# Weight differences tied to a later weight tile, and the last layer's value product as three 256-column matmuls

## The chip, the core and the metric

The kernel runs on one core of one Trainium2 chip. The metric is the device time of one launch in microseconds (us), the median of several executions. Engines are named as in the profile: PE (TensorE matmul) and PEld (its weight loads), DVE (VectorE), ACT (ScalarE), POOL (GpSimd), SP (SyncE, which issues the weight stream's DMAs).

## The reference

A two-layer encoder trunk over 272 tokens (16 meta tokens and 256 others) of width 2048, in float32. What matters here is the second half of each layer, the feed-forward part with inner width 5632:

```python
h2 = _rmsnorm(h_stream, norm_ffn[i])
up = h2 @ w_up[i]
u_gate = _dwconv3_centred(up[..., :D_FF], w_conv[i], b_conv[i])
u_val = up[..., D_FF:]
h_stream = h_stream + (jax.nn.silu(u_gate) * u_val) @ w_down[i]
```

The first half of a layer is grouped attention beside a Fourier branch, both gated and projected. The meta tokens are dropped at the end, so the last layer needs 256 columns of the value product.

## The kernel before, in words

**Precision.** Every float32 product is split in two parts. A weight tile `raw` (512 KB, four k-tiles by 256 output columns) is fetched by SP, copied on ACT into a rounded high part `wh` (the cast in `split_w`), and DVE subtracts to get the low part `wl`. The activations lie as a high and a low part too (`xHL`, `gHL`, `mH`/`mL`, `qH`/`qL`). One k-tile of one output tile is then three matmuls: `wh` by high, `wh` by low, `wl` by high. Activations are the moving operand of 272, 258 or 256 columns; 128 x 128 blocks of the weights are the stationary one, loaded anew by each matmul.

**Pairs.** Where high and low part together fit into 512 columns, `group` can issue two matmuls: `wh` by both parts side by side (512 columns) and `wl` by high (256 columns). The caller asks for it by handing over one moving operand in place of two. The two halves of the result then have to be added behind it. In the last layer (`fused`) the value product `uv` and the down products `d`, but for the last of them, are done like that.

**The stream.** `order` is a list of all weight tiles in the order of use. `advance` and `pump` keep the splits two tiles ahead of PE and the fetches four more. There are three buffers each for `wh` and `wl`, so the cast of tile i+2 can run when PE has finished tile i-1. A tile lasts 24 matmuls in a group of three. After every sixth matmul `step()` is called, four times a tile; it advances the side work, which is written as generators that say after how many steps they want to go on. All engines work their instructions off in the order in which the program was written.

**The weight sums.** For the last layer's down projection the first 32 of 44 k-tiles are done by a scheme with seven products per 2 x 2 block in place of eight. It needs differences of weight blocks, four for each of 16 block sets (`NPR`). The generator `weight_sums` makes them during the feed-forward part of layer 0: ACT issues a load of a 512 KB block into `b0` to `b3` (a one-element copy from the weight tile in use ahead of it ties it to that place in the stream), nine steps later DVE is given the subtraction, two steps later ACT is given the store into a DRAM tile `ts`. Layer 1 fetches the `ts` tiles back in its weight stream, and its products are called `ps_x`.

**Placement.** Tiles come from pools that are laid out one behind another: `per`, `wp`, `small`, and behind these `mix` (first half of a layer) and `ffn` (second half). The tables `X_AT`, `Q_AT`, `G_AT`, `FR_AT` and `WL_AT` say at which column within its tile a part begins.

Of the kernel before, what the change touches and what calls it, by code (L numbers as in the profile page):

```python
# [10 lines left out]
F32 = mybir.dt.float32  # L11
F32R = mybir.dt.float32r
AF = mybir.ActivationFunctionType
ALU = mybir.AluOpType
AX = mybir.AxisListType

P = 128
D = 2048
# [17 lines left out]
NPR = sum(FF_SPLIT[-1][:2]) // 2  # L36
# [17 lines left out]
X_AT, Q_AT, G_AT = ((44, 12), (24, 40)), ((44, 4), (8, 24)), ((12, 44), (0, 0))  # L54
# [1 line left out]
WL_AT.update({(0, k): 16 for k in ("q", "k", "v", "f", "f01", "ga", "gf", "ug", "uv", "d")})  # L56
FR_AT = 12
WL_AT.update({(l, "s"): 40 for l in range(2)})
WL_AT.update({(1, k): 16 for k in ("q", "ga", "gf", "a", "o", "ug")})
BLK = ((0, 16), (16, 144), (144, 272))  # L60

C_COS, C_SIN, C_MASK = 0, T, 2 * T
# [58 lines left out]
def encoder_kernel(ctx, tc, xT, params, consts, bmat, w_in, w_abr, w_four, w_f64, w_out, w_up, w_down, w_blk, outT):  # L121
    nc = tc.nc
# [98 lines left out]
    def split_w(i, a, b, eng=None):  # L221
        if i not in splits:
            h = wp.tile([P, CW, MG * P], F32R, tag="wh", name=f"wh{i}")
            lo = wp.tile([P, CW * MG * P + 64], F32R, tag="wl", name=f"wl{i}")
            o = wl_at[i]
            splits[i] = h, lo[:, o:o + CW * MG * P].rearrange("p (c m) -> p c m", c=CW)
        h, lo = splits[i]
        r = raws[i]
        if eng is None:
            nc.scalar.copy(h[:, a:b], r[:, a:b])  # L230
        else:
            eng.tensor_copy(h[:, a:b], r[:, a:b])
        nc.vector.tensor_tensor(lo[:, a:b], r[:, a:b], h[:, a:b].bitcast(F32), op=ALU.subtract)  # L233
        if b == CW:
            del raws[i]
# [283 lines left out]
    for l in range(DEPTH):  # L519
# [447 lines left out]
        with tc.tile_pool(name=f"ffn{l}", bufs=1) as fp:  # L967
# [2 lines left out]

            def weight_sums():
                tt = nc.vector.tensor_tensor
                for q in range(NPR):
                    b = [fp.tile([P, D // 2], F32, tag=f"b{e}", name=f"b{e}") for e in range(4)]
                    for e, sums in ((0, ()), (1, ((0, 1, 0, 0),)), (3, ((1, 3, 1, 1), (3, 3, 0, 2))), (2, ((2, 2, 3, 3),))):
                        nc.scalar.copy(b[e][:, 0:1], st["cur"][:, 0, 0:1].bitcast(F32))
                        nc.scalar.dma_start(b[e], w_blk[2 * q + e // 2, e % 2])
                        yield 9
                        for o, x, y, to in sums:
                            tt(b[o], b[x], b[y], op=ALU.subtract)  # L980
                            yield 2
                            nc.scalar.dma_start(tsum[q][to], b[o])
                        yield 3

            sets, prods = [], {"have": {}}
            if last:
# [83 lines left out]
            def both(t_, k, at):  # L1070
                a, n = at[0] + lo2, XP + at[1] - at[0]
                if n == XP:
                    return t_[:, k, :, a:a + W2]
                b = 2 * XP * k + a
                s = min(b, 2 * XP * t_.shape[1] - 2 * n)
                return t_.rearrange("p k r n -> p (k r n)")[:, s:s + 2 * n].rearrange("p (r n) -> p r n", r=2)[:, :, b - s:b - s + W2]

            k0 = 0
            for c, n in enumerate(FF_SPLIT[l]):
                whole = last and c < 2  # L1080
                if not last:
                    gHL = fp.tile([P, FF_SPLIT[l][0], 2, XP], F32R, tag="gHL", name="gHL")
                    gH, gL = (gHL[:, :, e, G_AT[l][e]:G_AT[l][e] + T] for e in range(2))
                    gp = lambda k: both(gHL, k, G_AT[l])
                elif whole:
                    gs = fp.tile([P, GN if c == 0 else n * SEQ], F32, tag=f"g{c}", name=f"g{c}")
                    sets.append(gs[:, :n * SEQ].rearrange("p (k t) -> p k t", t=SEQ))
                else:
                    gs = fp.tile([P, GN], F32R, tag="g0", name="gHL")[:, G_LAST:G_LAST + n * 2 * SEQ].rearrange("p (k e t) -> p k e t", e=2, t=SEQ)
                    gH, gL = gs[:, :, 0], gs[:, :, 1]  # L1090
                    gp = lambda k: gs[:, k]
                at_ = NM if last else 0
                if last and c:
                    push(combos(c - 1), 2)
                for i in range(k0 // MG, (k0 + n) // MG):
                    ps = group((l, "ug", i), xr(lo), W)
                    if i == 0:
                        drain()
                    cs = []
                    for m in range(MG):  # L1100
                        mt = 2 * i + m
                        wc = lambda t: prm[:, P_CW + (l * 3 + t) * FT + mt:P_CW + (l * 3 + t) * FT + mt + 1]
                        bc = prm[:, P_CB + l * FT + mt:P_CB + l * FT + mt + 1]
                        u = fp.tile([P, T], F32, tag="u", name="u", bufs=3)
                        nc.vector.tensor_tensor(u[:, lo:T], ps[m][:, :W], rstdB[:, lo:T], op=ALU.mult)
                        cv = fp.tile([P, T], F32, tag="cv", name="cv", bufs=4)
                        nc.scalar.activation(cv[:, lo2:T], u[:, lo2:T], AF.Identity, bias=bc, scale=wc(1))
                        a = max(lo2, 1)
                        nc.vector.scalar_tensor_tensor(cv[:, a:T], u[:, a - 1:T - 1], wc(0), cv[:, a:T], op0=ALU.mult, op1=ALU.add)
                        nc.vector.scalar_tensor_tensor(cv[:, lo2:T - 1], u[:, lo2 + 1:T], wc(2), cv[:, lo2:T - 1], op0=ALU.mult, op1=ALU.add)  # L1110
                        nc.scalar.activation(cv[:, lo2:T], cv[:, lo2:T], AF.Silu)
                        nc.vector.tensor_tensor(cv[:, lo2:T], cv[:, lo2:T], rstdB[:, lo2:T], op=ALU.mult)
                        cs.append(cv)
                    ps = group((l, "uv", i), (lambda kt: (both(xHL, kt, X_AT[l]),)) if fused else xr(lo2), W2)
                    for m in range(MG):
                        j = 2 * i + m - k0
                        cv = cs[m]
                        val = ps[m][:, :W2]
                        if fused:
                            v = fp.tile([P, W2], F32, tag="v", name="v", bufs=2)  # L1120
                            nc.scalar.copy(v, ps[m][:, W2:2 * W2])
                            nc.vector.tensor_tensor(v, v, val, op=ALU.add)
                            val = v
                        if whole:
                            nc.vector.tensor_tensor(sets[c][:, j, :], cv[:, lo2:T], val, op=ALU.mult)
                            continue
                        nc.vector.tensor_tensor(cv[:, lo2:T], cv[:, lo2:T], val, op=ALU.mult)
                        h_ = gH[:, j, lo2 - at_:T - at_]
                        nc.scalar.copy(h_, cv[:, lo2:T])
                        nc.vector.tensor_tensor(gL[:, j, lo2 - at_:T - at_], cv[:, lo2:T], h_.bitcast(F32), op=ALU.subtract)  # L1130
                lastc = c == len(FF_SPLIT[l]) - 1
                k0 += n
                if whole:
                    continue
                if last:
                    drain()
                    push(turned(), 2)
                for mg in range(8):
                    two = fused and not (lastc and mg == 7)
                    ps = group((l, "d", c, mg), (lambda kt: (gp(kt),)) if two  # L1140
                               else (lambda kt: (gH[:, kt, lo2 - at_:T - at_], gL[:, kt, lo2 - at_:T - at_])), W2)
                    if last and mg == 0:
                        drain()
                    for m in range(MG):
                        mt = 2 * mg + m
                        if two:
                            nc.vector.tensor_tensor(XT[:, mt, lo2:T], XT[:, mt, lo2:T], ps[m][:, W2:2 * W2], op=ALU.add)
                        if last and lastc:
                            ot = fp.tile([P, SEQ], F32, tag="ot", name="ot", bufs=3)
                            nc.vector.tensor_tensor(ot, XT[:, mt, NM:T], ps[m][:, :W2], op=ALU.add)  # L1150
                            nc.scalar.dma_start(outT[mt * P:(mt + 1) * P, :], ot)
                        else:
                            nc.vector.tensor_tensor(XT[:, mt, lo2:T], XT[:, mt, lo2:T], ps[m][:, :W2], op=ALU.add)
                            if lastc:
                                norm_in(mt, P_NM + (l + 1) * KT)
# [54 lines left out]
```

## Time and profile before

| what | value |
|---|---|
| time, median of 3 runs | 2530.25 us (2529.61 to 2532.1) |
| the profiled execution, its own time | 2528.11 us |
| its span | 2526.0 us |
| granted TensorE clock, mean | 0.999 |
| busy: PE, DVE, ACT | 99%, 73%, 51% |
| HBM traffic over the span | 218 GB/s |

PE's busy share counts matmuls that overlap in the pipeline, so it says that PE hardly ever has nothing to do, not that each matmul goes as fast as it can. What tells the speed of a run of matmuls is the distance from one start to the next. Start times in the timeline are in us from the start of the span; a duration there is that of one instruction from entering to leaving the engine, longer than that distance.

### The profile page before, as it was taken

To read this page: it belongs to the slowest core of one execution; us is meant where nothing else is said; L and a number is where in the kernel's file an instruction comes from. 1 tells how busy PE (TensorE), PEld (TensorE's weight loads), DVE (VectorE), ACT (ScalarE), POOL (GpSimd) and SP (SyncE) were. 2 spreads that over 40 slices of the span, in tenths; PEclk is the share of its full clock that TensorE was granted. 3 is DMA by queue.
4 is the path that set the end of the run, shared out by engine and by line. 5 is a ranking of instruction groups with operands and counts; after the bars stand their busy time and mean duration, and the time that the engine had idled before them with its cause. 6 is when DMAs were issued, how large, how long until landed. Compare 5 with 4: busy or idle time off the path is not lost.

```text
span 2526.0 us, 47879 instructions
## 1 busy us (share of the span) xinstructions
PE 2511.2 (99%) x19404; PEld 2441.2 (97%) x19404; DVE 1852.2 (73%) x2851; ACT 1276.4 (51%) x1857; POOL 18.3 (1%) x37
## 2 busy tenths in 40 slices
PE   9999999999999999999999999999999999999999
PEld 9999999999999999999999999999999989988888
DVE  7687867776776556676556887677766788879985
ACT  6455544554444334444444564445644565556653
POOL 0000000000000000000000000000000000000000
PEclk9999999999999999999999999999999999999999
DMA  7545666568888887787554555666656677778875
GB/s 240 166 157 161 194 185 190 189 225 283 286 282 281 277 292 266 270 288 266 183 179 151 175 157 188 196 201 200 188 189 192 217 243 247 244 249 256 260 244 174
DMA packets 157501, 557.63 MB, mean 221 GB/s; under 512 B 18144, under 2 KB 22112, under 8 KB 157280
## 3 DMA queue, kind: packets, MB, share of 16 engines
q1 hardware_dynamic: 134480, 482.54, 59.5%
q10 hardware_dynamic: 22800, 72.04, 8.1%
q8 instruction: 152, 2.49, 0.4%
q14 instruction: 69, 0.57, 0.1%
HBM read 516.07 MB, written 35.65 MB: 218 GB/s over the span
## 4 chain that ended last, share of the span: by engine, by line
PE 95%; DVE 2%; DMA 1%; ACT 1%; issue 1%; ACTq 0%; SPq 0%; DVEq 0%
PE ps_ug L306 6%; PE ps_ug L304 6%; PE ps_uv L300 6%; PE ps_ug L305 6%; PE ps_x L1046 6%; PE ps_d L306 4%; PE ps_d L304 4%; PE ps_d L305 4%; PE ps_uv L301 3%; PE ps_uv L306 3%; PE ps_uv L304 3%; PE ps_uv L305 3%; PE ps_o L304 2%; PE ps_o L306 2%; PE ps_o L305 2%; PE ps_gf L304 2%
## 5 line engine op out<-in xcount | busy, mean ns | idle before, releaser
L233 DVE TENSOR_TENSOR wl<-raw,wh 128x1024 fp32r<-128x1024 f32 (+1 forms) x883 | 1073.8, 1220 | 442.5 <-ACT wh L230 438.2
L230 ACT CAST wh<-raw 128x1024 fp32r<-128x1024 f32 (+1 forms) x882 | 920.9, 1046 | 853.6 <-PE ps_ug L305 171.4
L306 PE MATMUL ps_ug<-xHL,wl 128*128 128x272 f32 (+1 forms) x1408 | 397.6, 282 | 2.7 <-DVE wl L233 2.7
L304 PE MATMUL ps_ug<-xHL,wh 128*128 128x272 f32 (+1 forms) x1408 | 399.1, 283 | 0.0
L305 PE MATMUL ps_ug<-xHL,wh 128*128 128x272 f32 (+1 forms) x1408 | 397.1, 282 | 0.0
L306 PEld LDWEIGHTS ps_ug<-xHL,wl 128*128 128x128 f32 x1408 | 264.5, 188 | 3.1 <-DVE wl L233 3.1
L305 PEld LDWEIGHTS ps_ug<-xHL,wh 128*128 128x128 f32 x1408 | 264.8, 188 | 2.2
L304 PEld LDWEIGHTS ps_ug<-xHL,wh 128*128 128x128 f32 x1408 | 264.3, 188 | 2.7
L300 PE MATMUL ps_uv<-xHL,wh 128*128 128x512 f32 x704 | 247.7, 392 | 0.0
L306 PE MATMUL ps_d<-gHL,wl 128*128 128x272 f32 (+1 forms) x728 | 208.3, 286 | 2.5 <-DVE wl L233 2.5
L304 PE MATMUL ps_d<-gHL,wh 128*128 128x272 f32 (+1 forms) x728 | 208.8, 287 | 0.0
L305 PE MATMUL ps_d<-gHL,wh 128*128 128x272 f32 (+1 forms) x728 | 207.4, 285 | 0.0
L304 PE MATMUL ps_uv<-xHL,wh 128*128 128x272 f32 x704 | 201.3, 286 | 0.0
L306 PE MATMUL ps_uv<-xHL,wl 128*128 128x272 f32 x704 | 200.7, 285 | 0.0
L305 PE MATMUL ps_uv<-xHL,wh 128*128 128x272 f32 x704 | 199.9, 284 | 0.0
L301 PE MATMUL ps_uv<-xHL,wl 128*128 128x256 f32 x704 | 198.3, 282 | 0.0
L300 PEld LDWEIGHTS ps_uv<-xHL,wh 128*128 128x128 f32 x704 | 132.0, 188 | 28.6
L1046 PE MATMUL ps_x<-wh,cb 128*128 128x512 f32 x448 | 156.6, 393 | 0.0
L304 PE MATMUL ps_ga<-xHL,wh 128*128 128x272 f32 (+1 forms) x512 | 147.0, 287 | 0.0
L304 PE MATMUL ps_gf<-xHL,wh 128*128 128x272 f32 (+1 forms) x512 | 145.8, 285 | 0.1
L304 PE MATMUL ps_o<-mH,wh 128*128 128x272 f32 (+1 forms) x512 | 144.6, 282 | 0.0
L306 PE MATMUL ps_ga<-xHL,wl 128*128 128x272 f32 (+1 forms) x512 | 144.6, 282 | 0.0
(306 smaller groups left out, 5979.8 us busy)
## 6 DMA issues: line engine op xcount, KB each, us to landing
raw<-in_w_up SPq DMA_DIRECT2D x352, 512.0 KB, 4.4
raw<-in_w_in SPq DMA_DIRECT2D x206, 512.0 KB, 3.6
raw<-in_w_down SPq DMA_DIRECT2D x112, 512.0 KB, 4.3
raw<-in_w_out SPq DMA_DIRECT2D x64, 512.0 KB, 3.9
b<-in_w_blk ACTq DMA_DIRECT2D x64, 512.0 KB, 5.0
ts<-b ACTq DMA_DIRECT2D x64, 512.0 KB, 3.6
raw<-ts SPq DMA_DIRECT2D x64, 512.0 KB, 4.5
raw<-in_w_blk SPq DMA_DIRECT2D x48, 512.0 KB, 4.4
```

The costliest lines, as they stand in the source:

```text
L230: nc.scalar.copy(h[:, a:b], r[:, a:b])
L233: nc.vector.tensor_tensor(lo[:, a:b], r[:, a:b], h[:, a:b].bitcast(F32), op=ALU.subtract)
L300: nc.tensor.matmul(o2, h[:, c, sl], ab, start=kt == 0, stop=False)
L301: nc.tensor.matmul(o, lo[:, c, sl], ab[:, 0, :], start=False, stop=kt == nk - 1)
L304: nc.tensor.matmul(o, h[:, c, sl], a, start=kt == 0, stop=False)
L305: nc.tensor.matmul(o, h[:, c, sl], b, start=False, stop=False)
L306: nc.tensor.matmul(o, lo[:, c, sl], a, start=False, stop=kt == nk - 1)
L1046: nc.tensor.matmul(ps[e], cb[:, s_, q - q4], w, start=q == 0 and a == 0, stop=q == n - 1 and a == 2)
```

## The change

Three things are edited. `weight_sums` gives each subtraction to DVE not nine steps behind its load but in the slot of the next load, five steps into it, that is 17 steps behind its own. The subtraction becomes `scalar_tensor_tensor(x * one - y)`, where `one` is a new one-column tile of the pool `small` (two buffers): ACT makes it as 0 * w + 1 from the newest `wh` tile, so that the subtraction stands behind that tile's cast. The slots are 12 steps long each. Second, the last layer's `uv` product hands over two moving operands and so becomes three matmuls of 256 columns; the copy and the addition behind it go. Third, `wl` tiles of that product begin at column 16 like those of the neighbouring product `ug`.

```diff
-WL_AT.update({(1, k): 16 for k in ("q", "ga", "gf", "a", "o", "ug")})
+WL_AT.update({(1, k): 16 for k in ("q", "ga", "gf", "a", "o", "ug", "uv")})
...
+            st["new"] = h
             splits[i] = h, lo[:, o:o + CW * MG * P].rearrange("p (c m) -> p c m", c=CW)
...
-                for q in range(NPR):
-                    b = [fp.tile([P, D // 2], F32, tag=f"b{e}", name=f"b{e}") for e in range(4)]
+                b, due = {}, []
+                for q in range(NPR + 1):
                     for e, sums in ((0, ()), (1, ((0, 1, 0, 0),)), (3, ((1, 3, 1, 1), (3, 3, 0, 2))), (2, ((2, 2, 3, 3),))):
-                        nc.scalar.copy(b[e][:, 0:1], st["cur"][:, 0, 0:1].bitcast(F32))
-                        nc.scalar.dma_start(b[e], w_blk[2 * q + e // 2, e % 2])
-                        yield 9
-                        for o, x, y, to in sums:
-                            tt(b[o], b[x], b[y], op=ALU.subtract)
-                            yield 2
-                            nc.scalar.dma_start(tsum[q][to], b[o])
-                        yield 3
+                        if q < NPR:
+                            t_ = fp.tile([P, D // 2], F32, tag=f"b{e}", name=f"b{e}")
+                            nc.scalar.copy(t_[:, 0:1], st["cur"][:, 0, 0:1].bitcast(F32))
+                            nc.scalar.dma_start(t_, w_blk[2 * q + e // 2, e % 2])
+                        yield 5
+                        if due:
+                            one = small.tile([P, 1], F32, tag="one", name="one", bufs=2)
+                            nc.scalar.activation(one, st["new"][:, 0, 0:1].bitcast(F32), AF.Identity, bias=1.0, scale=0.0)
+                        for o, x, y, to in due:
+                            nc.vector.scalar_tensor_tensor(o, x, one, y, op0=ALU.mult, op1=ALU.subtract)
+                            yield 3
+                            nc.scalar.dma_start(to, o)
+                        if q == NPR:
+                            return
+                        b[e] = t_
+                        yield 7 - 3 * min(len(due), 2)
+                        due = [(b[o], b[x], b[y], tsum[q][to]) for o, x, y, to in sums]
...
-                    ps = group((l, "uv", i), (lambda kt: (both(xHL, kt, X_AT[l]),)) if fused else xr(lo2), W2)
+                    ps = group((l, "uv", i), xr(lo2), W2)
...
-                        if fused:
-                            v = fp.tile([P, W2], F32, tag="v", name="v", bufs=2)
-                            nc.scalar.copy(v, ps[m][:, W2:2 * W2])
-                            nc.vector.tensor_tensor(v, v, val, op=ALU.add)
-                            val = v
```

**ACT, the last set of weight sums (layer 0).** `b_...` are the block buffers, `ts_0` to `ts_3` the stores of the differences, `wh_...` the casts of the weight stream. Before, the second load of the set and what stands between it and the store that needs it:

```order
L977 DMA b_14160<-in_w_blk 128x1024
L230 CAST wh_14211<-raw_14067 128x1024
L230 CAST wh_14241<-raw_14097 128x1024
L982 DMA ts_0_117<-b_14159 128x1024
L230 CAST wh_14273<-raw_14128 128x1024
```

Now, the fourth load of the set and the store that needs it:

```order
L980 DMA b_13562<-in_w_blk 128x1024
L231 CAST wh_13509<-raw_13367 128x1024
L988 DMA ts_0_117<-b_13249 128x1024
L231 CAST wh_13540<-raw_13397 128x1024
L231 CAST wh_13573<-raw_13427 128x1024
L984 ACTIVATE one<-wh_13573 128x1
...
L231 CAST wh_13687<-raw_13532 128x1024
L1121 ACTIVATE cv<-cv 128x272
L984 ACTIVATE one<-wh_13687 128x1
L231 CAST wh_13720<-raw_13565 128x1024
L988 DMA ts_3_120<-b_13562 128x1024
```

Two casts stood between a load and the store of its difference; now it is seven, and one `one` stands ahead of each group of differences.

**DVE, the same set.** Before, the second and third difference (the first reads the third load):

```order
L233 TENSOR_TENSOR wl_14353<-raw_14203,wh_14352 128x1024
L1112 TENSOR_TENSOR cv<-cv,rstdB 128x272
L980 TENSOR_TENSOR b_14160<-b_14162,b_14160 128x1024
L233 TENSOR_TENSOR wl_14384<-raw_14233,wh_14383 128x1024
L980 TENSOR_TENSOR b_14162<-b_14162,b_14159 128x1024
L233 TENSOR_TENSOR wl_14416<-raw_14265,wh_14415 128x1024
```

Now the same two:

```order
L234 TENSOR_TENSOR wl_13574<-raw_13427,wh_13573 128x1024
L1115 TENSOR_TENSOR u<-ps_ug_0_13466,rstdB 128x272
L986 SCALAR_TENSOR_TENSOR b_13364<-b_13457,one,b_13364 128x1024
L1119 SCALAR_TENSOR_TENSOR cv<-u,prm,cv 128x271
...
L234 TENSOR_TENSOR wl_13625<-raw_13468,wh_13624 128x1024
L986 SCALAR_TENSOR_TENSOR b_13457<-b_13457,one,b_13249 128x1024
```

A difference still stands between two `wl` of the stream; it reads a load that was issued further back, and a scalar that ACT makes behind the cast of the tile whose `wl` stands just ahead.

**PE, a value product of the last layer.** The first k-tile of a product, behind the last matmul of a `ps_x` tile, before and now:

```order
L1046 MATMUL ps_x_25303<-wh_25588,cb 128x512
L300 MATMUL ps_uv_0_25653<-xHL,wh_25603 128x512
L301 MATMUL ps_uv_0_25653<-xHL,wl_25604 128x256
L300 MATMUL ps_uv_1_25654<-xHL,wh_25603 128x512
L301 MATMUL ps_uv_1_25654<-xHL,wl_25604 128x256
```

```order
L1056 MATMUL ps_x_25685<-wh_25996,cb 128x512
L305 MATMUL ps_uv_0_26061<-xHL,wh_26011 128x256
L306 MATMUL ps_uv_0_26061<-xHL,wh_26011 128x256
L307 MATMUL ps_uv_0_26061<-xHL,wl_26012 128x256
L305 MATMUL ps_uv_1_26062<-xHL,wh_26011 128x256
L306 MATMUL ps_uv_1_26062<-xHL,wh_26011 128x256
L307 MATMUL ps_uv_1_26062<-xHL,wl_26012 128x256
```

One k-tile of the two output tiles: four matmuls with 1536 columns have become six with the same 1536. For one output tile there are 704 such steps, in 22 groups of 32.

## The prediction

> **What bounds the kernel now.** The page comes first.
>
> ```profile
> span 2526.0 us, 47879 instructions
> PE 2511.2 (99%) x19404; PEld 2441.2 (97%) x19404; DVE 1852.2 (73%) x2851; ACT 1276.4 (51%) x1857; POOL 18.3 (1%) x37
> ```
>
> PE is busy for all but 15 us, so the end is the sum of the distances between matmul starts, and two things can move it: matmuls that follow each other faster or slower, and holes on PE. The holes are listed whole in the waits of PE (waited for: us in total, times, longest):
>
> ```profile
> PE ps_ug L306 <- DVE wl L233: 2.7, 2, 1.7
> PE ps_f L361 <- ACT wh L230: 2.5, 3, 1.6
> PE ps_d L306 <- DVE wl L233: 2.5, 1, 2.5
> PE ps_s L340 <- DVE wl L233: 1.8, 3, 0.8
> PE ps_idle L432 <- DVE ones L428: 1.1, 1, 1.1
> PE ps_pt L853 <- DVE pn L844: 0.8, 1, 0.8
> PE ps_ss L687 <- DVE sqm L780: 0.3, 1, 0.3
> ```
>
> No wait of `ps_uv` or `ps_x` is among them: in the last layer's feed-forward part PE waits for nobody. The first and third row are layer 0's feed-forward part, where the weight sums run. The waits of DVE and ACT say why a `wl` was late there:
>
> ```profile
> DVE b L980 <- DMA b<-in_w_blk: 69.3, 44, 4.9
> ACT wh L230 <- DVE b L980: 30.2, 8, 6.6
> ```
>
> Of 64 differences 44 reach DVE before their block has landed. DVE stands, and the `wl` queued behind the difference with it. ACT stands too, since the store in its queue waits for the difference, and the next cast is behind that store. Mostly the two tiles of lead absorb this. Three times they don't; the PE timeline has the matmul before and after each hole:
>
> ```profile
> 1016.50 0.28 PE L305 MATMUL ps_ug<-xHL,wh 128*128 128x272 f32 x1
> 1017.75 0.39 PE L306 MATMUL ps_ug<-xHL,wl 128*128 128x272 f32 x1 [0.96 <-DVE wl L233]
> ...
> 1070.55 0.28 PE L305 MATMUL ps_ug<-xHL,wh 128*128 128x272 f32 x1
> 1072.56 0.39 PE L306 MATMUL ps_ug<-xHL,wl 128*128 128x272 f32 x1 [1.73 <-DVE wl L233]
> ...
> 1184.03 0.28 PE L305 MATMUL ps_d<-gHL,wh 128*128 128x272 f32 x1
> 1186.77 0.39 PE L306 MATMUL ps_d<-gHL,wl 128*128 128x272 f32 x1 [2.46 <-DVE wl L233]
> ```
>
> The third one in the timelines of DVE and ACT:
>
> ```profile
> 1184.35 1.23 DVE L980 TENSOR_TENSOR b<-b,b 128x1024 f32<-128x1024 f32 x1 [4.86 <-DMA b<-in_w_blk]
> 1185.49 1.22 DVE L233 TENSOR_TENSOR wl<-raw,wh 128x1024 fp32r<-128x1024 f32 x1
> ```
>
> ```profile
> 1176.38 0.34 ACTq L977 DMA_DIRECT2D b<-in_w_blk  x1
> ...
> 1186.04 1.04 ACT L230 CAST wh<-raw 128x1024 fp32r<-128x1024 f32 x1 [6.63 <-DVE b L980]
> ```
>
> The load was issued at 1176.38 and its difference could start at 1184.35, 8 us later. After this hole the clock fell, as the windows show (PE with its count, then PEld, DVE, ACT, POOL, the granted clock, DMA share, GB/s):
>
> ```profile
> 1187.20:1191.20 4.00, 4.00 (x22) 4.00 (x21) 3.36 (x6) 1.78 (x4) 0.00 (x0) 0.57 0.93 299
> 1191.20:1195.20 4.00, 4.00 (x35) 4.00 (x35) 2.36 (x3) 2.09 (x2) 0.00 (x0) 1.00 0.97 358
> ```
>
> **The change part by part. The holes.** A matmul at full clock takes 4.00 / 35 = 0.114 us by the second window, which counts those at its edges too. Taking 0.12 off each distance, the holes are 1.25 - 0.12, 2.01 - 0.12 and 2.74 - 0.12, together 5.6 us. The slow clock lost 35 - 22 = 13 matmuls, 13 x 0.114 = 1.5 us. Sum 7.1 us. The Trainium skill ("TensorE: Matmul & The Clock Gate", What's actually happening) puts the fall to half clock behind an idle window of about 3.4 us. Here 2.46 us were enough, so the trace differs; by the Trainium skill alone the term would be 5.6 us.
>
> What does the new schedule leave of it? All rows on the blocks together:
>
> ```profile
> L976 ACT COPY b<-wh x64: 173/191/194, 532.9 to 1191.0; 128x1 f32<-128x1 f32 x64
> L980 DVE TENSOR_TENSOR b<-b,b x64: 1216/1226/1228, 547.4 to 1195.4; 128x1024 f32<-128x1024 f32 x64
> ...
> DMA to landing us min/median/max: 2.6/4.6/7.9
> ```
>
> A tile of the stream is 24 matmuls and four steps, so a step is 6 x 0.12 = 0.73 us. Before, a difference was queued 9 steps or 6.6 us behind its load, less than the 7.9 us of the slowest; hence the waits. Now it is 17 steps or 12.4 us, with 4.5 us in hand over the slowest landing. I take the whole 7.1 us as gained. At worst nothing goes, if another wait comes in.
>
> The new wait is for `one`. Behind the waiting difference on DVE stand the next `wl` and the feed-forward arithmetic. `one` is a one-column operation (191 ns for the like) and stands on ACT behind the cast whose `wl` DVE has just done or is about to do, so DVE hardly waits longer than for that cast. There are 48 of them, 9 us of ACT, which is busy for 51% of the span. The store now follows its difference by three steps in place of two, so ACT stands less. The loads come every 12 steps, four in 48 steps against 56: 17% denser.
>
> ```profile
> 860.00:1000.00 140.00, 140.00 (x1145) 139.83 (x1145) 85.05 (x95) 57.78 (x74) 0.00 (x0) 1.00 0.83 280
> ```
>
> The sums move 128 x 0.524 MB in 664 us, 101 GB/s; 118 would bring 280 to 297 and the DMA share from 0.83 to 0.88. The stream's fetches lead by four tiles (12 us), so I cost it at nothing; if that cover fails, it is the rival of the wait that comes back. A `scalar_tensor_tensor` is a little slower than a `tensor_tensor`; DVE has room.
>
> **The value product.** First and last starts give the distance per k-tile and output tile (32 in a group, 8 in a run between two `ps_x` tiles):
>
> ```profile
> 1815.98 0.39 PE L300 MATMUL ps_uv<-xHL,wh 128*128 128x512 f32 x1
> 1827.08 0.29 PE L304 MATMUL ps_ug<-xHL,wh 128*128 128x258 f32 x1
> 1838.22 0.39 PE L300 MATMUL ps_uv<-xHL,wh 128*128 128x512 f32 x1
> ...
> 2083.60 0.28 PE L304 MATMUL ps_ug<-xHL,wh 128*128 128x258 f32 x1
> 2086.45 0.39 PE L1046 MATMUL ps_x<-wh,cb 128*128 128x512 f32 x1
> ...
> 2096.32 0.39 PE L300 MATMUL ps_uv<-xHL,wh 128*128 128x512 f32 x1
> 2099.10 0.40 PE L1046 MATMUL ps_x<-wh,cb 128*128 128x512 f32 x1
> ...
> 2514.22 0.28 PE L304 MATMUL ps_d<-gHL,wh 128*128 128x256 f32 x1
> 2522.58 0.28 PE L306 MATMUL ps_d<-gHL,wl 128*128 128x256 f32 x1
> ```
>
> A pair takes (1827.08 - 1815.98) / 32 = 346.9 ns, a triple of `ug` with 258 columns (1838.22 - 1827.08) / 32 = 348.1. In the 14 later groups, mixed with `ps_x`, it is 2.78 / 8 = 347.5 for the pair and 2.85 / 8 = 356.3 for the triple: behind 512 columns, triples start slowly. The only triples with 256 columns, the last down product, take 3 x 8.36 / 71 = 353.2, at other columns of other tiles. So the work in columns is the same, and the pair gains from its fewer weight loads only behind `ps_x`.
>
> If the new product goes like `ug`: (348.1 - 346.9) x 256 + (356.3 - 347.5) x 448 = 0.3 + 3.9 = 4.2 us more. If it goes like the down product, with the 8.2 ns behind `ps_x` on top: (353.2 - 346.9) x 256 + (361.4 - 347.5) x 448 = 1.6 + 6.2 = 7.8. At the other end it costs nothing, if the slow start belongs to the columns at which `ug` begins. I take 4.2: `ug` has the same activations, the same weight column and the same neighbours. Two columns fewer speak for less, the down product for more. The Trainium skill ("TensorE: Matmul & The Clock Gate", Back-to-back issue gap) gives N/2.4 + 2.5 ns: 215.8 + 109.2 for the pair, 3 x 109.2 for the triple, an estimate of 2.6 ns a step or 1.8 us. All the rows above are longer than that.
>
> The copies and additions that go:
>
> ```profile
> L1121 ACT COPY v<-ps_uv x44: 358/371/374, 1825.9 to 2453.4; 128x256 f32<-128x256 f32 x44
> L1122 DVE TENSOR_TENSOR v<-v,ps_uv x44: 410/414/416, 1826.7 to 2455.0; 128x256 f32<-128x256 f32 x44
> ```
>
> 16 us of ACT and 18 us of DVE lie beside a PE that waits for neither there: worth nothing.
>
> **Columns.** The two buffers of `one` lie in `small`, and everything placed behind (`mix`, `ffn`) moves by 64 bytes, 16 columns. That touches the moving operand of 704 down steps, 128 + 256 branch and output steps in layer 0 and as many of the latter in layer 1: 1472 triples. Does the column matter? 353.2 against 348.1 for fewer columns says that it may, by 5.1 ns, 7.5 us in all. The same 7.5 us the other way is the lower bound, since no row says which pace a place gives. I take nothing: the shift keeps each operand's place within 64 bytes.
>
> Sum: -7.1 + 4.2 = -2.9 us, 2525.2 for the profiled execution (2528.11, its span and 2.1 around it). The median of the three runs is 2530.25, 2.1 above that execution; from it 2527.3.
>
> **The rivals.**
>
> *The product costs nothing.* The slow start of `ug` behind `ps_x` is peculiar to it, and 256 columns go at the pair's pace: -7.1 + 0.3, 2523.5. For it: equal columns, 1.2 ns difference in the unmixed groups. Against: 56 runs like 2083.60. The Trainium skill ("SBUF — State Buffer", Who interferes with whom) has PE waiting on nobody, and would exclude column effects; the 353.2 speaks against that.
>
> *The product goes like the down product.* -7.1 + 7.8, 2531.0.
>
> *Slower: the columns.* All 2176 triples that are new or moved go at the slow pace: -7.1 + 7.8 + 7.5 = +8.2, 2538.4. It decides the sign from 7.1 us of added time on, 3.3 ns a step, and passes the bound below from 12.2 us on, 5.6 ns a step. For it: the two paces of triples. Against: the moved steps keep their place within 64 bytes, as said.
>
> *The wait comes back.* DVE stands for `one`, or denser loads land later than 12 us: +4.2 with no hole gone, 2534.5. Against: 4.5 us in hand.
>
> **How the numbers follow.** A measurement of this kernel can tell about 0.2%, 5.1 us, from no change: 2525.2 to 2535.3. Forecast 0.40 (of which 0.12 beyond the bound, as two columns fewer save something), product free 0.24, slow product 0.13, columns 0.13, wait back 0.10 (0.01 of it beyond). Faster 0.36, same 0.50, slower 0.14. The range runs from 2522, under the free product, to 2536.5, short of the columns' full price.
>
> **What would show it.** Right: no row `DVE b <- DMA` of over 10 us in the waits, no PE hole between 530 and 1200, granted clock 1.00 there; `ps_uv` groups of 11.1 to 11.2 us before 1980 and runs of 2.85 us after. Wrong: groups of 11.3, down steps of layer 0 off their present pace, or DVE waiting for `one`.

## The result: slower, and the profile after

| | before | after |
|---|---|---|
| median of 20 runs each, us | 2526.54 (2520.53 to 2532.1) | 2534.22 (2533.26 to 2535.68) |
| ratio | | 1.0029 [1.0022, 1.0036] |
| span of the profiled execution, us | 2526.0 | 2532.3 |
| runs' spread, us | 11.6 | 2.4 |

The change costs 7.7 us, 0.29%, where 2.9 us less was forecast. The three runs known before it (2530.25) were 3.7 us above the median of twenty. The page after, and all waits of PE (waited for: us in total, times, longest):

```profile
span 2532.3 us, 49297 instructions
PE 2523.1 (100%) x20108; PEld 2481.6 (98%) x20108; DVE 1841.1 (73%) x2807; ACT 1267.5 (50%) x1861; POOL 18.3 (1%) x37
```

```profile
PE ps_f L362 <- ACT wh L231: 2.9, 4, 1.1
PE ps_s L341 <- DVE wl L234: 1.3, 3, 0.8
PE ps_idle L433 <- DVE ones L429: 1.1, 1, 1.1
PE ps_ss L688 <- DVE sqm L781: 0.3, 1, 0.3
```

The waits of `ps_ug` and `ps_d` in layer 0 are gone, and with them the stretch of slow clock behind the last of them: the mean granted clock went from 0.999 to 1.000. PE is busy all through, 20108 - 19404 = 704 matmuls more are the new triples, and still the span is longer. So the matmuls themselves follow each other more slowly. That shows where no instruction changed: layer 0's down product. A window of 100 us inside it, `ps_d` alone (PE, PEld and DVE busy with counts, granted clock, DMA share, GB/s), first before, then after:

```profile
1195.00:1295.00 100.00, 100.00 (x820) 100.00 (x820) 6.06 (x14) 1.00 0.58 188
```

```profile
1195.00:1295.00 100.00, 100.00 (x806) 100.00 (x805) 6.08 (x14) 1.00 0.58 177
```

The same work at the same clock without a hole: 100 us / 820 = 122.0 ns a matmul before, 100 / 806 = 124.1 after (a window also counts the matmuls that its edges cut, so such figures lie a little under the distance from start to start). The output projection of layer 1 (`ps_o`, 40 us, before and after) lost more, 114.9 to 119.4 ns:

```profile
1761.00:1801.00 40.00, 40.00 (x348) 40.00 (x348) 5.92 (x14) 1.00 0.64 195
```

```profile
1761.00:1801.00 40.00, 40.00 (x335) 40.00 (x335) 5.63 (x14) 1.00 0.63 185
```

The value product after, in the PE timeline (start, duration):

```profile
1829.71 0.28 PE L305 MATMUL ps_ug<-xHL,wh 128*128 128x258 f32 x1
1840.80 0.28 PE L305 MATMUL ps_uv<-xHL,wh 128*128 128x256 f32 x1
1852.11 0.28 PE L305 MATMUL ps_ug<-xHL,wh 128*128 128x258 f32 x1
...
2087.55 0.28 PE L305 MATMUL ps_ug<-xHL,wh 128*128 128x258 f32 x1
2090.34 0.40 PE L1056 MATMUL ps_x<-wh,cb 128*128 128x512 f32 x1
...
2100.13 0.28 PE L305 MATMUL ps_uv<-xHL,wh 128*128 128x256 f32 x1
2102.97 0.39 PE L1056 MATMUL ps_x<-wh,cb 128*128 128x512 f32 x1
```

Among themselves the new triples take (1852.11 - 1840.80) / 32 = 353.4 ns a step, `ug` with two columns more only (1840.80 - 1829.71) / 32 = 346.6. Behind `ps_x` a run of eight takes 2.84 us for `uv` and 2.79 for `ug`, where `ug` took 2.85 before.

The differences and their scalar, from the view of tile `b` and the waits between 530 and 1200 us:

```profile
L986 DVE SCALAR_TENSOR_TENSOR b<-b,one,b x64: 1274/1279/1285, 564.0 to 1111.4; 128x1024 f32<-128x1024 f32 x64
...
DMA to landing us min/median/max: 3.4/5.9/8.2
```

```profile
DVE b L986 <- ACT one L984: 3.0, 5, 0.6
```

No row of DVE waiting for a block is left; for `one` it waited five times, 3.0 us in all.

### The profile page after: what moved, and what is told of

Its sections match the earlier page's. It is cut to its first block, busy times and chain, and to the rows that moved or that the text cites. A ratio compares the mean times of both kernels' runs of the same rounds, so it can differ in the third digit from the quotient of the medians.

```text
span 2532.3 us, 49297 instructions
## 1 busy us (share of the span) xinstructions
PE 2523.1 (100%) x20108; PEld 2481.6 (98%) x20108; DVE 1841.1 (73%) x2807; ACT 1267.5 (50%) x1861; POOL 18.3 (1%) x37
## 4 chain that ended last, share of the span: by engine, by line
PE 97%; DVE 1%; ACT 1%; DMA 0%; issue 0%; SPq 0%; DVEq 0%; ACTq 0%
PE ps_uv L307 7%; PE ps_uv L305 7%; PE ps_uv L306 7%; PE ps_ug L305 7%; PE ps_ug L307 7%; PE ps_ug L306 7%; PE ps_x L1056 6%; PE ps_d L305 4%; PE ps_d L307 4%; PE ps_d L306 4%; PE ps_o L306 2%; PE ps_o L307 2%; PE ps_o L305 2%; PE ps_gf L305 2%; PE ps_gf L307 2%; PE ps_gf L306 2%
## 5 line engine op out<-in xcount | busy, mean ns | idle before, releaser
L305 PE MATMUL ps_uv<-xHL,wh 128*128 128x272 f32 (+1 forms) x1408 | 398.6, 283 | 0.0
L306 PE MATMUL ps_uv<-xHL,wh 128*128 128x272 f32 (+1 forms) x1408 | 397.4, 282 | 0.0
L307 PE MATMUL ps_uv<-xHL,wl 128*128 128x272 f32 (+1 forms) x1408 | 397.3, 282 | 0.0
L306 PEld LDWEIGHTS ps_uv<-xHL,wh 128*128 128x128 f32 x1408 | 264.7, 188 | 2.7
L305 PEld LDWEIGHTS ps_uv<-xHL,wh 128*128 128x128 f32 x1408 | 264.3, 188 | 2.4
L307 PEld LDWEIGHTS ps_uv<-xHL,wl 128*128 128x128 f32 x1408 | 264.4, 188 | 0.0
L306 PE MATMUL ps_o<-mL,wh 128*128 128x272 f32 (+1 forms) x512 | 146.2, 285 | 0.0
L307 PE MATMUL ps_o<-mH,wl 128*128 128x272 f32 (+1 forms) x512 | 145.7, 285 | 0.0
```

Of the source, the lines that this page charges most:

```text
L305: nc.tensor.matmul(o, h[:, c, sl], a, start=kt == 0, stop=False)
L306: nc.tensor.matmul(o, h[:, c, sl], b, start=False, stop=False)
L307: nc.tensor.matmul(o, lo[:, c, sl], a, start=False, stop=kt == nk - 1)
```

## The experiments

The runs were spread over three chips, each with runs of the kernel before beside them: the first four on one (the median of before there was 2527.42 us), the shifts by 16, 32 and 48 columns of the new sums and the first run with `cb` moved on the second (2527.75), the rest on the third (2527.76). These medians agree within 0.4 us. The theory at the start: the time is lost because the mixing and feed-forward tiles lie 16 columns further, as `one` takes 16 columns of `small`. The rivals: the triples alone, or the new order of the sums.

### The columns alone, the sums alone, the triples alone

The kernel before with an unused tile of 16 columns in `small`:

```diff
+    small.tile([P, 16], F32, name="pad", bufs=1)
```

> Before, with one unused tile of 16 float32 columns (64 bytes) in the pool small: every tile of mix and ffn moves as it does in the change, nothing else differs. Theory (columns): the down, branch and output triples get slower as in the trace after; d of layer 0 by about 8 ns a triple (5.6 us), a and o of layer 0 by 6 (2.5 us), of layer 1 by 13 (4.9 us), the last down pairs by 6 ns (1 us): +12 to +15 us over before, holes as before. Rival (the loss is the value product and the differences' wait): within 1 us of before.

2536.41 us (2533.69 to 2544.92), 1.0035 [1.0023, 1.0048]. Not one instruction differs, and 9.0 us are lost. That is less than the 12 to 15 expected, which put layer 0's `d` too high and left out that `ug` and `uv` gain; the sums over whole products further down give 10.6 for a move by 16 columns. The profiled execution was the slowest of the ten and had more holes than before's (waits of PE), so its span doesn't give the size; the pace of `ps_d` where it has no hole is that of after:

```profile
PE ps_ug L306 <- DVE wl L233: 4.7, 4, 2.6
PE ps_uv L306 <- DVE wl L233: 4.4, 4, 1.8
```

```profile
1210.00:1310.00 100.00, 100.00 (x806) 100.00 (x805) 6.08 (x14) 1.00 0.57 183
```

The new `weight_sums` alone (`uv` as pairs), `one` in a tile 32 wide, so that its two buffers move everything behind by 64 columns:

```diff
+                            one = small.tile([P, 32], F32, tag="one", name="one", bufs=2)[:, 0:1]
```

> The new weight sums alone, with the tile of ones 32 columns wide, so that its two buffers move all behind them by 256 bytes and every column keeps its place within 256 bytes; value product as pairs. Theory (the holes were worth their 7.1 us, columns are the loss): 5 to 7 us faster than the median before, about 2520, no PE hole between 530 and 1200. Rival (the wait for one, or the denser loads, cost): not faster than before.

2520.92 us (2518.97 to 2522.23), 0.9972 [0.9962, 0.9981]: 6.5 us less than before. The waits on `wl` in the feed-forward part are gone, and the pace is before's:

```profile
1195.00:1295.00 100.00, 100.00 (x820) 100.00 (x819) 6.07 (x14) 1.00 0.55 180
```

The triples alone on the kernel before (`uv` with two moving operands, its `wl` at column 16, the old sums):

```diff
-WL_AT.update({(1, k): 16 for k in ("q", "ga", "gf", "a", "o", "ug")})
+WL_AT.update({(1, k): 16 for k in ("q", "ga", "gf", "a", "o", "ug", "uv")})
...
+                    ps = group((l, "uv", i), xr(lo2), W2)
...
```

> Before with the value product as triples alone (weight column 16, no ones, no move). Theory: the triples cost 3.8 us in uv, and ug behind them wins back 2.8 since no 512-column matmul precedes it: +1 to +3 us. Rival (triples at the slow pace are the main loss): +7 us or more.

2528.93 us (2522.32 to 2533.77), 1.0005 [0.9994, 1.0016]. The holes vary by more than the effect, from run to run; by the medians the sign stays open here. In the trace its `uv` matmuls take 248.9 us in all against 245.3, and `ug`, `uv` and `ps_x` of the last layer together 651.3 against 648.6: 2.7 us more.

The whole change with the 32-wide `one`:

```diff
-                            one = small.tile([P, 1], F32, tag="one", name="one", bufs=2)
+                            one = small.tile([P, 32], F32, tag="one", name="one", bufs=2)[:, 0:1]
```

> The whole change, with the tile of ones 32 columns wide in place of one, so that all columns keep their place within 256 bytes. Theory (columns): 2520 to 2523, the change without its columns' loss, 11 to 14 us faster than the change. Rival (columns do not matter): as the change, 2534.

2521.76 us (2520.14 to 2522.46), 0.9974 [0.9965, 0.9982]. One number in a tile's shape turns 0.29% slower into 0.26% faster, 12.5 us apart. Beside the sums alone, the triples cost 0.8 us here by the medians, 2.6 by the traces (651.2 against 648.6).

### How far, and which way

The new sums with `one` as the change has it (16 columns), pairs kept; then the sums with 64 columns and an unused tile of 32 or 48 more:

```diff
+                            one = small.tile([P, 1], F32, tag="one", name="one", bufs=2)
```

> The new weight sums with the tile of ones as in the change (two buffers of 64 bytes in all, so everything behind moves by 16 columns), value product as pairs. Beside the kernel with 64 columns it differs in the place of the tiles alone, and neither has holes. Theory (columns; terms from the two traces per product: d 4.7 and a, o 2.5 in layer 0, a, o 5.0, d 0.9, ps_x 1.3 in layer 1, less 2.8 for ug and 1.0 for uv behind ps_x): 10 to 11 us above that kernel, 2531 to 2532. Rival (the padded tile of ones helped in another way than by columns): within 2 us of it, 2521 to 2523.

```diff
+    small.tile([P, 32], F32, name="pad", bufs=1)
```

> The new weight sums with the tile of ones 64 columns in all and an unused tile of 32 columns: everything in mix and ffn moves by 128 bytes against the kernel without it. Theory A (the pace depends on the column modulo 32): as that kernel, 2520 to 2522. Theory B (modulo 64): slower, 2524 or more, each product by its own amount. Theory C (distance from the kernel's tables is not what counts, 16 columns were a chance hit): faster for some products and slower for others.

```diff
+    small.tile([P, 48], F32, name="pad", bufs=1)
```

> As the last, with 48 columns. Theory A (modulo 32): as the move by 16, 2531 to 2532, with the same terms for each product. Theory B (modulo 64): terms of its own, d of layer 0 as with 16 since its two parts then lie at 28 and 60 in place of 60 and 28 (both move, the low-part product with them).

Measured: 2529.73 (1.0008 [0.9999, 1.0018]), 2531.6 (1.0017 [1.0007, 1.0028]) and 2536.93 us (1.0039 [1.0026, 1.0052]). Against the 2520.92 of the sums alone, on another chip, 16 columns cost 8.8 us, 32 cost 10.7, 48 cost 16.0. The windows of `ps_d`, in this order:

```profile
1195.00:1295.00 100.00, 100.00 (x806) 100.00 (x805) 6.08 (x14) 1.00 0.54 175
```

```profile
1195.00:1295.00 100.00, 100.00 (x798) 100.00 (x798) 6.08 (x14) 1.00 0.55 174
```

```profile
1195.00:1295.00 100.00, 100.00 (x792) 100.00 (x791) 6.09 (x14) 1.00 0.54 173
```

The place within 64 bytes, on which the prediction relied, is kept by all three. A first theory of the cause, that the distance from the weights counts modulo 32 columns, would have had 32 columns cost nothing; it fell. The expectation that 48 columns would leave layer 0's `d` as 16 do fell as well: 792 matmuls in place of 806. 64 columns do cost nothing. Added over whole products (from each matmul's end to the next one's in the PE timeline, holes cut to the median; us; `d` of layer 0 before holds 1.6 us of slow clock):

```
shift in columns         before    64    16    32    48
d of layer 0              259.7  258.1  262.8  265.2  267.5
a + o of layer 0          141.2  141.2  143.7  143.6  143.6
a + o of layer 1          133.5  133.5  138.5  136.0  138.3
d of layer 1               65.8   65.8   66.7   67.3   66.8
ug, uv and ps_x           648.6  648.6  646.1  647.7  648.4
```

Every product has its own order of good and bad places; the last row even gains by 16.

### Together, or one alone

The sums with 64 columns, and an unused tile of 16 columns ahead of everything, so that weights, activations and all other tiles move together; and one of 16 columns at the start of the `ffn` pool of layer 0 only, where of the operands only `gHL` moves:

```diff
+    per.tile([P, 16], F32, name="pad")
```

> The new weight sums with columns kept, and an unused tile of 16 columns ahead of all tiles: activations, weights and everything else move by 64 bytes together. Theory R (what counts is where the moving operand lies against the weights loaded beside it): as without it, 2520 to 2522. Theory M (the moving operand's own column decides): d, a, o slower as in the change by 4.7, 2.5, 5.0 us, and ug, uv of both layers with them, 2531 or more.

```diff
+            if not last:
+                fp.tile([P, 16], F32, name="pad")
```

> The new weight sums with columns kept, and an unused tile of 16 columns at the start of the ffn pool of layer 0 alone: of the operands of PE only gHL moves, so only the down product of layer 0. Theory (terms add up, each from its own tile): 4.7 us slower than without, 2525 to 2526, all other products as without. Rival (the loss needs the moves together, or comes from DVE's and ACT's operands): within 1 us, 2520 to 2522.

Moved together: 2519.01 us (0.9967 [0.9955, 0.9979]), nothing lost. `gHL` alone: 2524.43 (0.9983 [0.9974, 0.9992]), 5.4 us more on the same chip. The windows of `ps_d`, together first, then `gHL` alone, and below that its `ps_o` of layer 1:

```profile
1195.00:1295.00 100.00, 100.00 (x820) 100.00 (x819) 6.08 (x14) 1.00 0.57 180
```

```profile
1195.00:1295.00 100.00, 100.00 (x806) 100.00 (x805) 6.08 (x14) 1.00 0.56 177
...
1755.00:1795.00 40.00, 40.00 (x348) 40.00 (x348) 5.92 (x14) 1.00 0.62 192
```

Only the moved product is slower: 806 in place of 820 in layer 0's `d`, its 348 kept in `o`. By the sum over `d` (262.8 against 258.1 us) that is 4.7 of the 5.4. So the column as such doesn't matter; the moving operand's place relative to the other tiles does. A moved tile of another engine is not the cause: in that window of the run with `gHL` alone moved, DVE and ACT work on `raw`, `wh`, `wl`, `xHL`, `XT`, `acc`, `sq` and `prm`, and the weight DMAs fill `raw`, none of which moved. Which of the tiles that stayed the operand has to be seen against, the weights that PE loads beside it or another, isn't separated.

### The value product again, and a better kernel

The 16 columns had made `ug` faster. In the last layer they also move `cb`. It is the stationary operand of `ps_x`: there the 512 columns of the weights are the moving one. The sums with 64 columns, and `cb` alone 16 columns further in its tile, with pairs, then with pairs whose `wl` begins at column 16, then with the triples of the change:

```diff
+                cbf = fp.tile([P, 8 * P + 64], F32R, tag="cb", name="cb", bufs=3)
+                cb = cbf[:, 16:16 + 8 * P].rearrange("p (a m t) -> p a m t", a=2, m=4)
```

> The new weight sums with all columns kept, but the split sums cb (the stationary operand of ps_x) begin 16 columns later in their tile, all else in place. Theory (ug starts slowly behind ps_x because of where cb lies, as the trace after shows with cb moved: ug 2.8 us and uv 1.0 us less, ps_x 1.3 more): 2.0 to 2.8 us faster than the kernel without it, 2518 to 2519. Rival (the gain of ug came from the triples or from another tile): no change.

> The fastest so far (new sums, columns kept, cb moved by 16) with the wl tiles of the last layer's uv product at column 16, as pairs. The down pairs, whose wl lie at that column, take 341 ns a pair and the uv pairs 347. If the weight column is what sets them apart: up to 6 ns x 704 = 4 us faster, 2514. If it is the activations' column: no change, 2518.

> The whole change with columns kept and cb moved by 16: beside the kernel with pairs it is the value product as triples alone, with no slow start behind ps_x for ug. From the traces uv takes 248.9 us as triples and 244.5 as pairs: about 4 us slower than with pairs, 2521 to 2523. Rival (triples are free, their cost was the start behind ps_x): as with pairs, 2518.

Measured: 2518.11 us (0.9961 [0.9947, 0.9976]), 2519.11 (0.9966 [0.9954, 0.9979]) and 2521.94 (0.9982 [0.9973, 0.9992]). The first is the fastest median of all and beats both kernels. The run of `ug` behind `ps_x` in the PE timeline, `cb` in its old place (sums alone), and 16 columns further:

```profile
2081.75 0.28 PE L305 MATMUL ps_ug<-xHL,wh 128*128 128x258 f32 x1
2084.60 0.39 PE L1056 MATMUL ps_x<-wh,cb 128*128 128x512 f32 x1
```

```profile
2083.75 0.28 PE L305 MATMUL ps_ug<-xHL,wh 128*128 128x258 f32 x1
2086.54 0.40 PE L1057 MATMUL ps_x<-wh,cb 128*128 128x512 f32 x1
```

2.85 us became 2.79: the slow start of `ug` hung on where `cb` lies. It is a start indeed: over all such runs, the first fourteen distances average 120.5 ns with `cb` in its old place and 116.6 with it moved, the last ten 115.9 in both. Over the last layer `ug` gains 2.8 us, `uv` 0.7, and `ps_x` loses 1.3; the medians differ by 2.8, on two chips. The second of these runs brought none of the up to 4 us held possible: the pair with the moved `wl` keeps its pace. The third shows the triples dearer than the pairs, by 3.8 us over the first (another chip) and by 2.8 over the second (same chip), from which the triples alone set it apart. With triples, where `cb` lies makes no difference to the sum: `ug`, `uv` and `ps_x` take 651.1 us together here, 651.2 in the kernel after and 651.2 with the 32-wide `one`, against 648.6 for pairs with `cb` in its old place and 646.4 in the new one.

## Why the prediction was right or wrong

**Holes: right.** -7.1 was forecast, -6.5 [-9.6 to -4.8 by the interval of the ratio] measured by the sums alone. The mechanism shows too: no `DVE b <- DMA`, no hole on `wl` in the feed-forward part, clock 1.00, and a spread of the runs of 2.4 us in place of 11.6. The slowest landing is now 8.2 us, far within 12.4. The new wait for `one` is what was said of it, 3.0 us on DVE and none on PE.

**Value product: right in size by luck, wrong in its parts.** +4.2 was forecast; after against the sums moved alike gives 2534.22 - 2529.73 = 4.5 us (in other runs), the trace 5.1. But the forecast took the columns as kept, and with them kept the triples cost 0.8 us by the medians and 2.6 by the traces. It was composed as `ug`'s pace (0.3) with `ug`'s slow start behind `ps_x` (3.9). Measured, the slow start is gone in both and the triples go at 353.4 ns from the first group, close to the 353.2 of the last down product. That row was quoted and put second, since activations and neighbours were `ug`'s. Nor was "behind 512 columns, triples start slowly" the right reading of 2.85: in the kernel after, `ug` stands behind the same 512 columns and starts at its pace, since `cb` moved; with triples and `cb` in its old place (the 32-wide `one`) its run still takes 2087.24 - 2084.39 = 2.85 us.

**Columns: the step that failed.** The prediction says: "I take nothing: the shift keeps each operand's place within 64 bytes." No row said that 64 bytes are what counts, and the runs with 32 and 48 columns show that they aren't: 64 columns, 256 bytes, leave every pace as it was, 16, 32 and 48 don't. What the step left out measured 8.8 us by medians (the sums with 16 against 64 columns) and 10.6 by the traces: 4.7 in `d` of layer 0, 2.5 and 5.0 in the branch and output products of layers 0 and 1, 0.9 in `d` of layer 1, 1.3 in `ps_x`, less 2.8 in `ug` and 1.0 in `uv`. The bound failed too. 5.1 ns a triple came from two rows that differ in columns and in other things too; the triples of `o` in layer 1 lost 3 x (119.4 - 114.9) = 13.5 ns. And the list of what moves was short: it left out `cb` and the down pairs of layer 1.

**The sum.** -6.5 + 8.8 + 4.5 = 6.8, with the traces' terms for the last two -6.5 + 10.6 + 5.1 = 9.2; measured 7.7. The first of these sums is no test: its medians form a chain, so it comes to the difference of the ends, 2534.22 - 2527.42, by itself. The rival of the columns had the sign and the cause; its 8.2 us came from a slow product (7.8, where 4.5 was measured) and 7.5 for the columns (8.8), so that its sum came near is luck in part. It got 0.13, on an argument that was no row. The Trainium skill ("SBUF — State Buffer", Who interferes with whom) gives PE two independent read ports, for the moving operand and for the weight load, and has only the pair that DVE and GpSimd share contend. By that the place of an operand would cost nothing, and the trace disagrees: 806 against 820 of the same matmuls in 100 us, where of the operands `gHL` alone was moved. Whether the two reads of PE contend is not shown.

**Open.** Why a place is good or bad. That weights and moving operand meet in the same part of memory would fit that places relative to each other count and that 256 bytes leave the pace as it was, but it is only a guess; what else is read beside them wasn't separated, and no rule gave the order of places of each product in advance. How the place of `cb` reaches the product behind it is open too. The sign of the triples alone on the kernel before stays open within its interval by the medians; the 2.7 us are the trace's.

## What to carry to other kernels

A new tile, however small, moves all that is allocated behind it: give it a size that keeps the places of matmul operands modulo 64 float32 columns, which was free in this kernel, or measure the shift alone with an unused tile before crediting the edit with the time. In a kernel bound by PE, count the matmuls in an equal window of a product that wasn't edited; a count that changes without a hole or a clock change is a reason to test the placement by itself. Two rows that differ in several things give neither the size nor a bound of one of them.

## What was not expected of the hardware

The distance between float32r matmuls depended on the place of their operands relative to the other tiles: 122.0, 124.1, 125.3 and 126.3 ns for the same `ps_d` matmuls when all behind `small` lay 0, 16, 32 and 48 columns further (100 us over 820, 806, 798, 792); for 16 columns the move of the moving operand alone gave the same 806. The place of one product's stationary operand can set the pace of the next one: with `cb` 16 columns further, `ug` behind `ps_x` went from 2.85 to 2.79 us for 24 matmuls.
